# Mixture of experts: weights applied at the eviction, adding gathers, stores on ScalarE's queue, one loop for the rare blocks

## The chip, the cores and the metric

The kernel runs on one core of a Trainium2 chip. The metric is the time of one execution on the device in microseconds (us), the median of three runs. Beside the runs there is one profiled execution, from which all rows below are taken. TensorE (PE in the profile, PEld for its weight loads), VectorE (DVE), ScalarE (ACT), GpSimd (POOL) and SyncE (SP) run their own instruction streams; a small q behind a name (PEq, SPq) is an engine's sequencer, which takes branches and issues transfers.

## The reference, cut to what matters

Two layers of a model with three sequence mixers and a mixture of experts. The mixers and the projections before and after them don't change. The mixture of experts in each layer picks two of 32 experts for each token, runs them, and adds their results with weights; its input is adaptively normalised, and its sum is gated by a row g2 of the stream and added to ALPHA times the row before it goes through a layer norm. Layer 0 has 512 tokens of two streams, layer 1 has 256 of one.

```python
    weights = jax.nn.softmax(top_logit, -1) * group_w
    expert_id = group_idx[:, None] * EXPERTS_PER_GROUP + top_idx.astype(jnp.int32)
    ...
    def run_block(args):
        tok, e = args
        xb = h_pad[tok]
        hid = jax.nn.silu(xb @ w1[e]) * (xb @ w3[e])
        return hid @ w2[e]

    y = lax.map(run_block, (slot_tok.reshape(n_blocks, MOE_BLOCK), block_expert))
    y = y.reshape(cap, d).astype(F32) * slot_w[:, None]
    return jnp.zeros((n_tok + 1, d), F32).at[slot_tok].add(y)[:n_tok].astype(h.dtype)
```

## The kernel before

The tokens' assignments to experts, two for each token, are sorted by expert into slots (1024 in layer 0, 512 in layer 1). `permute` builds one-hot matrices on VectorE and GpSimd and multiplies by them, so that the normalised rows stand in slot order, transposed, in `XS`. `pos` is a slot's number, `posi` the row of the scratch tensor `ysD` in DRAM in which that slot's result lies; `ysD` has NR parts, which the experts take in turn.

An expert works on blocks of RB = 64 slots. `expert_steps` gives the steps of a block: `rows` copies the block's columns of `XS` to `xt`, `up` multiplies them with w1 and w3 (L1616), `gate` is Silu and a product (L1621, L1622), `turn` transposes the result on TensorE (L110, copied by L1628), `down` multiplies with w2 (L1636). `down` then copies the result from PSUM to `yo` on ScalarE (L1638) and stores it to `ysD` by a transfer that GpSimd issues (L1639). `expert_block` is all steps of one block in a row. `e` runs over the experts in a loop that is written out, with the first half of the next expert's `up` moved ahead of `turn` and `down`; expert 0 has code of its own ahead of it.

How many slots an expert has is known only at run time, so the engines load the count (L1653) and branch. Every expert runs one block. `If(cnt > RB)` (L1721) guards a second block written out, and in it `If(cnt > 2 * RB)` (L1724) guards a loop for the rest (L1725). Of the 62 experts behind expert 0 in the two layers, 4 have more than 64 slots here, none more than 128. Behind the If, `reload(e)` issues on SP's queue the loads (L1356) of the weights that go into the buffers which expert e has left free; an expert has six pieces of 1 MB, and some fifteen pieces are held.

Behind the last expert, GpSimd fetches each token's two results by indirect gathers into `yg` (L1738). ScalarE multiplies the first by its weight (L1742), VectorE adds the second times its weight (L1745), GpSimd or VectorE multiplies by the gate row (L1746), VectorE adds ALPHA times the row X (L1747), and `normalise` works on pairs of 128-token blocks (L377 to L384). In layer 0 the next layer's mixers follow: TensorE transposes the rows (L110). The first three loads of their weights are held back by `late`, on ScalarE's queue, until the combination of block 2. In layer 1 the final norm and the store of the output follow.

Of the kernel before, what the change touches and what calls it, by code (L numbers as in the profile page):

```python
# [10 lines left out]
F32 = mybir.dt.float32  # L11
# [70 lines left out]
def backbone(ctx: ExitStack, tc: tile.TileContext, a, out, dbg=None, upto=None):  # L82
# [75 lines left out]
    late = {"n": 0, "ins": None}  # L158
# [253 lines left out]
    for l in range(NLAYER):  # L412
# [5 lines left out]
        late["n"] = 3 if l else 0  # L418
# [1005 lines left out]
        wgt = pe.tile([P, 2, nb], F32, name="wgt")  # L1424
# [28 lines left out]
        for s in streams:  # L1453
# [10 lines left out]
            ls_ = pr.tile([P, CTX], F32, name="ls", tag="o1", bufs=2)  # L1464
# [73 lines left out]
        def permute(q):  # L1538

            on = pr.tile([P, nb, QT], F32R, name="on", tag="on", bufs=2)  # L1540
            for b in range(nb):
                o1 = pr.tile([P, QT], F32, name="o1", tag="o1", bufs=2)
                eng = nc.gpsimd if b % 2 else nc.vector
                eng.tensor_scalar(o1, io, posq[:, 0, b, q:q + 1], None, op0=OP.is_equal)
                nc.vector.scalar_tensor_tensor(on[:, b], io, posq[:, 1, b, q:q + 1], o1, op0=OP.is_equal, op1=OP.add)
            for kp in range(0, KD, 2):
                ps = ps_tile([P, 2, QT], "pj")
                for i in range(2):
                    for b in range(nb):
                        for x in range(2):  # L1550
                            mm(ps[:, i], h2r[(b0 + b) // 2, kp + i][x][:, b % 2], on[:, b], start=(b == 0 and x == 0),
# [6 lines left out]

        for b in blocks:
# [12 lines left out]
        for i in range(2):  # L1572
# [3 lines left out]
            nc.vector.tensor_add(posi[:, i], pos[:, i], rofs)  # L1576

# [10 lines left out]
        nc.vector.tensor_mul(wgt[:, 0], gw, den)  # L1588
        nc.vector.tensor_mul(wgt[:, 1], wgt[:, 0], e2)

        WHY = "a slot is counted once, so start and count stay within the slots"
        def block_tiles(px, tag, n, ny, static=0):

            return {k: px.tile(shp, F32, name=k, tag=tag + k, bufs=ny if k == "yo" else n)
                    for k, shp in (("xt", [P, KD, RB]), ("hd", [P, 256]), ("hh", [P, 2, P]), ("yo", [P, 512]))[static:]}

        def expert_steps(tl, e, off, piece=None):
# [4 lines left out]
            grp = [slice(g * RB, (g + 1) * RB) for g in range(2)]  # L1602
            t = {}

# [14 lines left out]
            def gate():  # L1619
                hd = tl["hd"]  # L1620
# [3 lines left out]
            def turn():  # L1624
                pt = ps_tile([P, 2, P])
                for j in range(2):
                    transpose(pt[:, j], tl["hd"][:, j::2])
                nc.vector.tensor_copy(tl["hh"], pt)  # L1628

            def down():  # L1630
                py = ps_tile([P, 512], "pj")
                for f in range(2):
                    for j in range(2):
                        k = 2 * f + j
                        for g in range(2):
                            mm(py[grp[g]], tl["hh"][:, j, grp[f]], w2(k, g * 512, 512), start=(k == 0), stop=(k == 3),  # L1636
# [144 lines left out]
```

## Time and profile before

| | us |
|---|---|
| runs, median of 3 (lowest to highest) | 2803.15 (2794.74 to 2810.39) |
| profiled execution, time | 2788.21 |
| its span | 2786.6 |
| PE, DVE, ACT, POOL busy | 2209.7, 1158.0, 664.0, 612.6 |
| TensorE's granted clock, mean | 0.905 |

The span is from the first to the last instruction that the profiler saw. Busy time of an engine is the sum over its instructions; two engines' busy times overlap. A row of a timeline gives start, duration, engine, line, operation, output and input, and in brackets the engine's idle time before it with what ended it.

### The profile page before, as it was taken

The numbers are of one execution on the slowest core, as the hardware profiler recorded it, in microseconds if no ns is written. First come the engines' busy times: TensorE is split into PE (matmuls) and PEld (weight loads), VectorE is DVE, ScalarE is ACT, GpSimd is POOL, SyncE is SP. The second block draws the span as 40 slices with busy tenths as digits, with TensorE's granted clock in tenths as the row PEclk, the third lists the DMA queues.
The fourth block names the chain that finished last, engine by engine and source line by source line (L and its number), as shares of the span: only waits on it lengthen the run. The fifth ranks groups of instructions, "written<-read, shape, count | busy, mean of one in ns | idle before, by whom it ended". The sixth has DMA issues, their size and how long they took to land. (4 is left out here: it accounts for less than half of the span.)

```text
span 2786.6 us, 42100 instructions
## 1 busy us (share of the span) xinstructions
PE 2209.7 (79%) x16239; PEld 1551.1 (56%) x16239; DVE 1158.0 (42%) x2451; ACT 664.0 (24%) x1308; POOL 612.6 (22%) x542
## 2 busy tenths in 40 slices
PE   7998988888898887777773899986878687678773
PEld 3666975677685644334331576874777443344331
DVE  4749445876456100000003779467864300000002
ACT  2421345443422100000001342345433100000000
POOL 1242110544333000000002242223554200000001
PEclk9998999999999999899887899998988898898886
DMA  9475451323765488999996258343357769999994
GB/s 316 153 215 171 130 167 42 100 76 103 206 213 197 176 345 318 362 408 408 353 382 219 62 164 262 112 154 87 92 167 241 291 248 381 352 400 408 407 389 157
DMA packets 350438, 657.22 MB, mean 236 GB/s; under 512 B 73462, under 2 KB 253214, under 8 KB 306808
## 3 DMA queue, kind: packets, MB, share of 16 engines
q1 hardware_dynamic: 287890, 599.97, 59.4%
q0 software_dynamic: 38160, 24.63, 2.9%
q10 hardware_dynamic: 24022, 27.84, 2.9%
q8 instruction: 218, 3.57, 0.5%
q14 instruction: 148, 1.21, 0.1%
HBM read 593.09 MB, written 59.02 MB: 234 GB/s over the span
## 5 line engine op out<-in xcount | busy, mean ns | idle before, releaser
L1616 PE MATMUL ps<-we,xt 128*64 128x256 f32 x4224 | 569.6, 423 | 240.5 <-PEq L1721 147.4
L1616 PEld LDWEIGHTS ps<-we,xt 128*64 128x64 f32 x4224 | 339.0, 152 | 458.2 <-issue 329.0
L209 PE MATMUL ps<-hT,whi 128*128 128x512 f32 (+2 forms) x880 | 327.1, 372 | 2.1 <-ACT whi L152 1.9
L154 POOL TENSOR_TENSOR wlo<-raw,whi 128x1024 fp32r<-128x1024 f32 (+1 forms) x84 | 206.2, 2455 | 543.6 <-ACT whi L152 453.2
L211 PE MATMUL ps<-hT,wlo 128*128 128x512 f32 (+2 forms) x880 | 317.2, 360 | 0.3 <-DVE wlo L154 0.3
L210 PE MATMUL ps<-hT,whi 128*128 128x512 f32 (+2 forms) x880 | 317.3, 361 | 0.0
L1639 POOL DMA_DIRECT2D ysD<-yo x69 | 55.6, 806 | 1074.7 <-ACT yo L1638 954.0
L1636 PE MATMUL ps<-we,hh 128*64 128x512 f32 x1104 | 251.9, 597 | 5.2 <-DVE hh L1628 2.6
L152 ACT ACTIVATE whi<-raw 128x1024 fp32r<-128x1024 f32 x174 | 180.1, 1044 | 221.9 <-PE ps L210 158.9
L1638 ACT ACTIVATE yo<-ps 128x512 f32<-128x512 f32 x69 | 41.2, 597 | 798.7 <-PE ps L1636 769.9
L1610 DVE COPY xt<-XS 128x512 f32 x66 | 28.2, 427 | 483.2 <-PE ps L1616 479.0
L1628 DVE COPY hh<-ps 128x256 f32<-128x256 f32 x69 | 29.3, 425 | 409.7 <-PE ps L110 409.7
L209 PEld LDWEIGHTS ps<-hT,whi 128*128 128x128 f32 (+1 forms) x880 | 172.0, 195 | 42.4 <-issue 12.6
L211 PEld LDWEIGHTS ps<-hT,wlo 128*128 128x128 f32 (+1 forms) x880 | 171.4, 195 | 31.4 <-issue 6.9
L210 PEld LDWEIGHTS ps<-hT,whi 128*128 128x128 f32 (+1 forms) x880 | 171.9, 195 | 25.0 <-issue 3.3
L154 DVE TENSOR_TENSOR wlo<-raw,whi 128x1024 fp32r<-128x1024 f32 x90 | 148.1, 1647 | 44.6 <-ACT whi L152 38.8
L1636 PEld LDWEIGHTS ps<-we,hh 128*64 128x64 f32 x1104 | 79.5, 138 | 135.2 <-issue 118.8
L210 PE MATMUL ps<-wlo,hT 128*128 128x256 f32 x384 | 110.1, 287 | 1.5 <-DVE wlo L154 1.5
L209 PE MATMUL ps<-whi,hT 128*128 128x256 f32 x384 | 110.9, 289 | 0.0
L211 PE MATMUL ps<-whi,hT 128*128 128x256 f32 x384 | 109.7, 286 | 0.0
L288 PE MATMUL ps<-wmod,sT 128*32 128x256 f32 x768 | 90.0, 521 | 14.0 <-DMA wmod<-in_w_mod 11.5
L1621 ACT ACTIVATE hd<-ps 128x256 f32<-128x256 f32 x69 | 26.4, 383 | 249.9 <-PE ps L1616 249.9
(423 smaller groups left out, 3718.6 us busy)
## 6 DMA issues: line engine op xcount, KB each, us to landing
we<-in_w SPq DMA_DIRECT2D x338, 1024.0 KB
raw<-in_w_in SPq DMA_DIRECT2D x121, 512.0 KB
wmod<-in_w_mod SPq DMA_DIRECT2D x96, 512.0 KB
we<-in_w SPq DMA_DIRECT2D x92, 512.0 KB
ysD<-yo POOLq DMA_DIRECT2D x69, 256.0 KB, 16.2
ysD<-X SPq DMA_DIRECT2D x17, 512.0 KB
raw<-in_w_out SPq DMA_DIRECT2D x16, 512.0 KB
mgD<-st ACTq DMA_DIRECT2D x24, 256.0 KB
```

The costliest lines, as they stand in the source:

```text
L152: nc.scalar.activation(hr[:, :, off:off + pn], rv, AF.Copy)
L154: eng.tensor_sub(lr[:, :, off:off + pn], rv, hr[:, :, off:off + pn])
L209: mm(ps, st[0](k), mv[0](k), start=(k == 0), stop=False)
L210: mm(ps, st[0](k), mv[1](k), start=False, stop=False)
L211: mm(ps, st[1](k), mv[0](k), start=False, stop=(k == kt - 1))
L288: mm(hold["ps"][32 * j:32 * j + 32, :], sT[:, k, :], cols, start=(k == 0), stop=(k == KD - 1 and v not in mod_d[l]))
L1610: nc.vector.tensor_copy(t["xt"], XS[:, :, ds(off, RB)])
L1616: mm(t["ph"][grp[g], i], t["xt"][:, k], (w1, w3)[i](k, g * 256, 256), start=(k == 0), stop=(k == KD - 1), tile_position=(0, g * RB))
L1628: nc.vector.tensor_copy(tl["hh"], pt)
L1636: mm(py[grp[g]], tl["hh"][:, j, grp[f]], w2(k, g * 512, 512), start=(k == 0), stop=(k == 3), tile_position=(0, g * RB))
L1638: nc.scalar.activation(tl["yo"], py, AF.Copy)
L1639: nc.gpsimd.dma_start(ysD[e % NR, ds(off, RB)].rearrange("s (g c) -> g s c", g=2), tl["yo"])
```

## The change

Four edits, all in the mixture of experts.

1. Each slot's weight is written to a scratch tensor `wsD` in DRAM by indirect transfers of GpSimd, one for each 128 tokens and choice (8 in layer 0, 4 in layer 1), with a zero tail. In layer 0 a slot has two weights, one for each stream, one of them zero. Each block loads its 64 weights twice, to both halves of `wc`, on ScalarE's queue.
2. `down` multiplies by the weight and by the gate row g2 on VectorE where the result leaves PSUM (in layer 0 once for each stream, and adds the two), and the store to `ysD` is issued by ScalarE.
3. The gathers add their rows to X in the transfer itself, first all first choices, then all second ones. ALPHA goes into the rows of the norm that makes X. The combination on ScalarE, VectorE and GpSimd is gone, `late` with it.
4. The second block and the loop behind it become one loop over all blocks beyond the first.

```diff
-            if late["n"]:
-                late["n"] -= 1
-                with tc.issue_after(late["ins"]):
-                    nc.scalar.dma_start(dst, v)
-            else:
-                nc.sync.dma_start(dst, v)
+            nc.sync.dma_start(dst, v)
...
+        wsD = dram.tile([ns + RB, nst], F32, name=f"wsD{l}")
+        g2 = [pe.tile([P, 512], F32, name=f"g2_{s}") for s in streams]
...
+        nc.gpsimd.tensor_scalar(lnrow, lnrow, ALPHA, None, op0=OP.mult)
...
+        nc.scalar.dma_start(wsD[ns:ns + RB], XS[0:RB, 0, ns:ns + nst])
+        for i in range(2):
+            for b in range(nb):
+                nc.gpsimd.indirect_dma_start(out=wsD, out_offset=bass.IndirectOffsetOnAxis(ap=posw[:, i, b:b + 1], axis=0),
+                                             in_=wgt[:, i, b], in_offset=None)
...
+            def weights():
+                for g in range(2):
+                    nc.scalar.dma_start(tl["wc"][grp[g]], wsD[ds(off, RB)])
...
-                nc.scalar.activation(tl["yo"], py, AF.Copy)
-                nc.gpsimd.dma_start(ysD[e % NR, ds(off, RB)].rearrange("s (g c) -> g s c", g=2), tl["yo"])
+                for x in range(nst):
+                    nc.vector.scalar_tensor_tensor(tl["hd" if x else "yo"], py, tl["wc"][:, x:x + 1], g2[x], op0=OP.mult,
+                                                   op1=OP.mult)
+                if nst > 1:
+                    nc.vector.tensor_add(tl["yo"], tl["yo"], tl["hd"])
+                nc.scalar.dma_start(ysD[e % NR, ds(off, RB)].rearrange("s (g c) -> g s c", g=2), tl["yo"])
...
             with tc.If(cnt > RB, label=f"beyond{l}_{e}", preferred_fallthrough_block=True):
-                to = block_tiles(px, *ZO)
-                expert_block(to, e, more(off + RB))
-                with tc.If(cnt > 2 * RB):
-                    with tc.For_i(2 * RB, cnt, RB) as i:
-                        expert_block(to, e, more(off + i))
+                with tc.For_i(RB, cnt, RB) as i:
+                    expert_block(block_tiles(px, *ZO), e, more(off + i))
             reload(e)
...
-            ins = nc.scalar.activation(y0, y0, AF.Copy, scale=wgt[:, 0, b:b + 1])
-            if b == 2:
-                late["ins"] = ins.ins
-            nc.vector.scalar_tensor_tensor(y0, y1, wgt[:, 1, b:b + 1], y0, op0=OP.mult, op1=OP.add)
-            (nc.vector if b == nb - 1 else nc.gpsimd).tensor_mul(y0, y0, g2[(b0 + b) // 2])
-            nc.vector.scalar_tensor_tensor(X[:, b0 + b], X[:, b0 + b], ALPHA, y0, op0=OP.mult, op1=OP.add)
-            if b % 2:
-                normalise([b0 + b - 1, b0 + b])
+        for i in range(2):
+            for b in range(nb):
+                nc.gpsimd.indirect_dma_start(out=X[:, b0 + b], out_offset=None, in_=ysD.rearrange("r s c -> (r s) c"),
+                                             in_offset=bass.IndirectOffsetOnAxis(ap=posi[:, i, b:b + 1], axis=0),
+                                             compute_op=OP.add)
+        for b in range(0, nb, 2):
+            normalise([b0 + b, b0 + b + 1])
```

How the streams stand to each other is seen at three places. The first is GpSimd in the routing stage of layer 0, in the changed kernel, with what each instruction waits for: `on` are the one-hot matrices of `permute`, DMASW0 to DMASW6 are the semaphores of GpSimd's own transfers, in the order of their issue.

```order
L1599 DMA wsD_7579<-wgt,posw 1088x2 [waits DMAHW6_49,DVE_49]
L1599 DMA wsD_7579<-wgt,posw 1088x2 [waits DMASW0_49]
L1542 TENSOR_SCALAR on<-io,posq 128x256 [waits PE_49]
L1599 DMA wsD_7579<-wgt,posw 1088x2 [waits DMASW1_49,DVE_49]
L1542 TENSOR_SCALAR on<-io,posq 128x256 [waits PE_49]
L1599 DMA wsD_7579<-wgt,posw 1088x2 [waits DMASW2_49]
L1599 DMA wsD_7579<-wgt,posw 1088x2 [waits DMASW3_49,DVE_49]
L1599 DMA wsD_7579<-wgt,posw 1088x2 [waits DMASW4_49]
```

These transfers are new. Each waits for the one issued before it, and two one-hot matrices stand between them.

The second is ScalarE at the first block of layer 0, in the changed kernel: L1687 are the branches for expert 0's rare blocks, DMASW7 is the semaphore of the last of those eight transfers.

```order
L1687 COMPARE_AND_BRANCH
L1621 DMA wc<-wsD_7579 64x2 [waits DMAHW5_49,DMASW7_49]
L1621 DMA wc<-wsD_7579 64x2 [waits DMAHW6_49]
L1638 ACT_TABLE_LOAD
L1638 ACTIVATE hd<-ps 128x256 [waits PE_49]
L1661 DMA ysD<-yo 2x64x512 [waits DMAHW7_49,DVE_49]
```

The two loads of weights and their waits now stand ahead of the table load and the Silu; the copy `yo` is gone from this queue and the store has come to it.

The third is the branch behind an expert. First TensorE in the kernel before, from the load of the count to the end of the loop's matmuls:

```order
L1653 TENSOR_LOAD cnt_i
L1721 COMPARE_AND_BRANCH
L1616 MATMUL ps<-we,xt 64x256 x32
L110 MATMUL ps<-cst,hd 128x128 x2
L1636 MATMUL ps<-we,hh 64x512 x8
L1724 COMPARE_AND_BRANCH
L1725 COMPARE_AND_BRANCH
L1725 UNCONDITIONAL_BRANCH x2
L1777 BRANCH_PREFETCH_HINT
L1616 MATMUL ps<-we,xt 64x256 x32
L110 MATMUL ps<-cst,hd 128x128 x2
L1636 MATMUL ps<-we,hh 64x512 x8
```

And in the changed kernel:

```order
L1676 TENSOR_LOAD cnt_i
L1746 COMPARE_AND_BRANCH
L1747 COMPARE_AND_BRANCH
L1747 UNCONDITIONAL_BRANCH x2
L1790 BRANCH_PREFETCH_HINT
L1634 MATMUL ps<-we,xt 64x256 x32
L110 MATMUL ps<-cst,hd 128x128 x2
L1653 MATMUL ps<-we,hd 64x512 x8
L1747 REGISTER_ALU
L1747 COMPARE_AND_BRANCH
L1747 UNCONDITIONAL_BRANCH
L1746 UNCONDITIONAL_BRANCH
```

One copy of a block is gone from between the branch and its target, and the second block of an expert is now reached through the entry of a loop. On SP the same entry of the loop, in the changed kernel, reads as follows; the second row lists all queues' semaphores (DMASW of GpSimd's, DMAHW of SP's and ScalarE's) and those of the engines:

```order
L1746 COMPARE_AND_BRANCH
L1747 COMPARE_AND_BRANCH
L1747 UNCONDITIONAL_BRANCH [waits DMAHW2_49,DMAHW3_49,DMAHW4_49]
L1747 UNCONDITIONAL_BRANCH [waits DMASW4_49,DMASW3_49,DMASW5_49,DMASW2_49,DMASW6_49,DMASW1_49,DMASW7_49,DMASW0_49,DMAHW0_49,SP_sequencer_49,DMAHW1_49,DVE_sequencer_49,DMAHW2_49,PE_sequencer_49,DMAHW3_49,Activation_sequencer_49,DMAHW4_49
L1790 BRANCH_PREFETCH_HINT
L1747 REGISTER_ALU
L1747 COMPARE_AND_BRANCH
```

A loop of this form stood in the kernel before too (L1725), behind two branches; it is not entered there with these counts, and it is now entered four times.

## Rows read from the trace of the kernel before

**Rows 1.** Table of stretches: us, busy PE PEld DVE ACT POOL, PEclk, DMA share, GB/s
```profile
900.00:940.00 40.00, 36.35 (x281) 25.84 (x281) 7.12 (x15) 5.43 (x9) 5.38 (x8) 1.00 0.50 190
1060.00:1180.00 120.00, 87.05 (x557) 45.20 (x556) 8.82 (x21) 6.86 (x14) 5.59 (x7) 0.87 0.95 370
1180.00:1305.00 125.00, 95.57 (x646) 50.65 (x648) 9.25 (x22) 7.46 (x15) 6.37 (x8) 0.92 1.02 407
1305.00:1435.00 130.00, 93.95 (x586) 48.74 (x584) 8.82 (x21) 6.86 (x14) 5.58 (x7) 0.83 0.93 366
2330.00:2475.00 145.00, 105.99 (x684) 55.56 (x682) 9.67 (x23) 8.44 (x17) 7.17 (x9) 0.87 0.93 365
```

**Rows 2.** The line of the branch: durations in ns, then who waited
```profile
L1721 PEldq COMPARE_BRANCH  x62: 70/3387/7289, 966.8 to 2738.4; - x62
...
  PE ps L1616: 159.0, 38
```

**Rows 3.** Timeline of TensorE, layer 0, behind a long branch
```profile
1348.67 3.68 PE L1616 MATMUL ps<-we,xt 128*64 128x256 f32 x16 [5.25 <-PEq L1721]
```

**Rows 4.** Timeline of the fronts of both layers
```profile
891.53 0.15 DVE L1589 TENSOR_TENSOR wgt<-wgt,e 128x4 f32<-128x4 f32 x1
...
907.04 0.38 ACT L1621 ACTIVATE hd<-ps 128x256 f32<-128x256 f32 x1 [9.54 <-PE ps L1616]
...
2188.47 2.37 DVE L1589 TENSOR_TENSOR wgt<-wgt,e 128x2 f32<-128x2 f32 x1
...
2203.45 0.38 ACT L1621 ACTIVATE hd<-ps 128x256 f32<-128x256 f32 x1 [9.48 <-PE ps L1616]
```

**Rows 5.** The line of the gathers, us from issue to landing
```profile
DMA to landing us min/median/max: 4.3/5.7/6.5
```

**Rows 6.** Timeline, start of layer 1's mixers
```profile
1531.77 0.43 SPq L124 DMA_DIRECT2D db<-in_gdn_dt_bias  x1
...
1534.03 1.28 ACT L551 ACT_TABLE_LOAD   x1 [9.08 <-DMA db<-in_gdn_dt_bias]
```

**Rows 7.** Timeline of TensorE around three blocks beyond 64 slots
```profile
998.76 7.13 PE L1616 MATMUL ps<-we,xt 128*64 128x256 f32 x64 [1.64 <-DVE xt L1610]
...
1044.03 7.13 PE L1616 MATMUL ps<-we,xt 128*64 128x256 f32 x64 [1.97 <-DVE xt L1610]
...
1057.72 1.95 PE L1616 MATMUL ps<-we,xt 128*64 128x256 f32 x16 [0.96 <-ACTq L1724]
...
2275.90 7.13 PE L1616 MATMUL ps<-we,xt 128*64 128x256 f32 x64 [1.63 <-DVE xt L1610]
```

**Rows 8.** Table of stretches around those blocks
```profile
1000.00:1010.00 10.00, 8.55 (x68) 5.42 (x66) 0.85 (x2) 0.38 (x1) 0.00 (x0) 1.00 0.42 161
...
1040.00:1050.00 10.00, 8.03 (x76) 5.92 (x74) 1.26 (x3) 0.38 (x1) 0.40 (x1) 1.00 0.65 258
...
2280.00:2290.00 10.00, 7.89 (x55) 4.04 (x51) 0.85 (x2) 0.98 (x2) 0.38 (x1) 1.00 0.54 204
```

**Rows 9.** The line of the stores, us from issue to landing
```profile
DMA to landing us min/median/max: 8.6/16.2/21.2
```

**Rows 10.** Timeline of the end of layer 0
```profile
1490.22 0.80 POOL L1639 DMA_DIRECT2D ysD<-yo  x1 [9.38 <-ACTq L1721]
1500.40 1.07 POOL L1738 DMA_INDIRECT yg<-ysD,posi  x1 [9.38 <-issue]
...
1538.07 3.93 PE L110 MATMUL ps<-cst,X 128*128 128x128 f32 x16 [48.83 <-DVE X L384]
```

**Rows 11.** Timeline of the end of layer 1
```profile
2743.85 0.80 POOL L1639 DMA_DIRECT2D ysD<-yo  x1 [10.70 <-ACTq L1721]
...
2755.74 1.05 POOL L1738 DMA_INDIRECT yg<-ysD,posi  x1 [11.10 <-DMA ysD<-yo]
...
2768.57 0.69 DVE L377 BATCH_NORM_STATS2 bst<-X 128x6 f32<-128x512 f32 x1
...
2776.27 1.53 DVE L384 TENSOR_SCALAR X<-X,bve,bnm 128x1024 f32<-128x1024 f32 x2
```

More of the change, by code (lines that the diff above doesn't have):

```diff
@@ L1538, in permute @@
         def permute(q):
-            on = pr.tile([P, nb, QT], F32R, name="on", tag="on", bufs=2)
+            on = [pr.tile([P, QT], F32R, name="on", tag="on", bufs=nb + 2) for _ in range(nb)]
             for b in range(nb):
-                o1 = pr.tile([P, QT], F32, name="o1", tag="o1", bufs=2)
                 eng = nc.gpsimd if b % 2 else nc.vector
-                eng.tensor_scalar(o1, io, posq[:, 0, b, q:q + 1], None, op0=OP.is_equal)
-                nc.vector.scalar_tensor_tensor(on[:, b], io, posq[:, 1, b, q:q + 1], o1, op0=OP.is_equal, op1=OP.add)
+                eng.tensor_scalar(on[b], io, posq[:, 0, b, q:q + 1], None, op0=OP.is_equal)
+                nc.vector.scalar_tensor_tensor(on[b], io, posq[:, 1, b, q:q + 1], on[b], op0=OP.is_equal, op1=OP.add)
             for kp in range(0, KD, 2):
@@ L1550, in permute @@
                         for x in range(2):
-                            mm(ps[:, i], h2r[(b0 + b) // 2, kp + i][x][:, b % 2], on[:, b], start=(b == 0 and x == 0),
+                            mm(ps[:, i], h2r[(b0 + b) // 2, kp + i][x][:, b % 2], on[b], start=(b == 0 and x == 0),
                                stop=(b == nb - 1 and x == 1))
@@ L1576, in backbone @@
             nc.vector.tensor_add(posi[:, i], pos[:, i], rofs)
+        posw = pr.tile([P, 2, nb], I32, name="posw")
+        nc.vector.tensor_copy(posw, pos)
+        wgt = pr.tile([P, 2, nb, nst], F32, name="wgt")
+        nc.gpsimd.memset(wgt, 0.0)
+        own = [wgt[:, i, 2 * x:2 * x + 2, x] for i in range(2) for x in range(nst)]
         eg = pr.tile([P, nb, NG], F32, name="eg")
@@ L1602, in expert_steps @@
             grp = [slice(g * RB, (g + 1) * RB) for g in range(2)]
+            hd, hh = tl["hd"][:, :256], tl["hd"][:, 256:].rearrange("p (j s) -> p j s", j=2)
             t = {}
+            def weights():
+                for g in range(2):
+                    nc.scalar.dma_start(tl["wc"][grp[g]], wsD[ds(off, RB)])
             def rows():
@@ L1626, in turn @@
                 for j in range(2):
[L1627 to L1628 removed]
+                    transpose(pt[:, j], hd[:, j::2])
+                nc.vector.tensor_copy(hh, pt)
             def down():
@@ L1635, in down @@
                         for g in range(2):
-                            mm(py[grp[g]], tl["hh"][:, j, grp[f]], w2(k, g * 512, 512), start=(k == 0), stop=(k == 3),
+                            mm(py[grp[g]], hh[:, j, grp[f]], w2(k, g * 512, 512), start=(k == 0), stop=(k == 3),
                                tile_position=(0, g * RB))
-                nc.scalar.activation(tl["yo"], py, AF.Copy)
-                nc.gpsimd.dma_start(ysD[e % NR, ds(off, RB)].rearrange("s (g c) -> g s c", g=2), tl["yo"])
-            return rows, up, gate, turn, down
+                for x in range(nst):
+                    nc.vector.scalar_tensor_tensor(tl["hd" if x else "yo"], py, tl["wc"][:, x:x + 1], g2[x], op0=OP.mult,
[3 more added lines that the diff above has]
+                nc.scalar.dma_start(ysD[e % NR, ds(off, RB)].rearrange("s (g c) -> g s c", g=2), tl["yo"])
+            return rows, up, gate, turn, down, weights
         def expert_block(*args):
-            rows, up, gate, turn, down = expert_steps(*args)
+            rows, up, gate, turn, down, weights = expert_steps(*args)
+            weights()
             rows()
@@ L1705, in backbone @@
         for e in range(1, NE):
-            rows, up, gate, turn, down = steps.pop(e)
+            rows, up, gate, turn, down, _ = steps.pop(e)
             tc.mark_branch_hint_location(f"beyond{l}_{e}", "LikelyTaken")
```

30 lines of the change are left out of this document (12 added, 18 removed).

## The prediction

> **What bounds the kernel now.** The expert stage runs from about 900 to 1490 us in layer 0 and from 2190 to 2745 us in layer 1, so it is two fifths of the time, and all of the change lies in it and at its two ends. I read the table of stretches first [rows 1]. In 1180 to 1305 the DMA share is 1.02 at 407 GB/s: that is the ceiling, and the experts' weights set the pace there. In 1060 to 1180 the share is 0.95, in 1305 to 1435 0.93, in 2330 to 2475 0.93, so there something else holds the loads up for a part of the time. What it is, the line of the branch tells [rows 2]: TensorE's branch behind each expert took 0.07 us at best, 3.4 in the median and 7.3 at worst, on the same test each time, and the next expert's matmuls waited 159 us for it. In the long case TensorE sits idle 5.25 us and its next 16 matmuls take 3.68 us [rows 3], against 1.95 for 16 such matmuls in a run that is not interrupted [rows 7]: it comes back slower, and the granted clock of the stretch is 0.83 against 0.92 where the loads set the pace [rows 1]. The branch is taken over code that is not run, and what is jumped over is the block beyond 64 and the loop behind it, two copies of a block. That one and the same test takes so differently long says that the code at the target is sometimes at hand and sometimes has to be brought.
>
> The two ends are chains of waits: last result, store, gathers, combination, normalisation, and TensorE idle over all of it, 48.83 us behind layer 0 [rows 10] and to the end of the program behind layer 1 [rows 11]. The front is a chain too: routing, weights, first block [rows 4].
>
> **The change part by part.** The profiled execution took 2788.2 us, the median of the runs is 2803.15, 0.5% above. I add up differences on the profile and put them on the median.
>
> *Weights by slot (front of each layer).* After the weights are known (VectorE, 891.7 us [rows 4]), GpSimd writes them to DRAM with 8 indirect transfers in layer 0 and 4 in layer 1. Each waits for the one before it to land, as the order shows, since all write one tensor. ScalarE's load of the first block's weights waits for the last of them, and behind that load on ScalarE's queue stand the table load and the first Silu, for which all of TensorE waits. No row has such a transfer. From below a small transfer of the hardware queue, 1531.77 to 1534.03, 2.3 us [rows 6]; from above the indirect gathers, 4.3 to 6.5 us [rows 5]. It moves 8 bytes a row where the gather moves 4 KB, so I take 3.8, just under the shortest gather. Layer 0: 891.7 + 8 x 3.8 = 922.1, two loads issued at about 0.4 each [rows 6] and a table load of about 1.3 behind it: Silu at 924 in place of 907.04, **+17** (2.3 us each: +5; 5.7 each: +32). Layer 1: 2190.8 + 4 x 3.8 = 2206 + 2 = 2208 against 2203.45 [rows 4]: **+4.5** (0 to +12). It is not made up later: the DMA share in 900 to 940 is 0.50 [rows 1], that is, the weights prefetched are in their buffers and nothing can be loaded until an expert is done.
>
> *The multiplication where the results leave PSUM.* One copy on ScalarE becomes three operations on VectorE in layer 0, one in layer 1. At 0.69 us for 128x512 [rows 11] that is 2.1 us. VectorE is busy 9 of 120 us [rows 1], and the next matmuls into that bank come an expert later: nothing, but for the last block, where it adds 1.5 us ahead of the store (counted below). The scaling of the norm's row by GpSimd and the earlier loads of the gate's rows lie in the routing stage, in which GpSimd waits; nothing. The first loads of layer 1 on SP's queue: nothing, since SP has issued all experts by then.
>
> *The loop for slots beyond 64.* It is run 4 times here: twice in layer 0 (from 998.76 and 1044.03), twice in layer 1 (one at 2275.90) [rows 7]. Now such a block is straight code; after one of them TensorE stood idle 0.96 us [rows 7]. In the changed kernel it is the body of a loop, and the order shows at its entry and its exit a wait of SP for the semaphores of all DMA queues and all engines, and a release of all engines together. At the entry SP waits until the weights under way have landed. They kept the DMA engines busy 4.2 us from 1000, 6.5 us from 1040 and 5.4 us from 2280 [rows 8], which is up to 5.4, 2.5 and 9.5 us after the blocks' starts; for the fourth I count none: 17 in all. At the exit the block's store has to land (2.3 to 8.6 us [rows 6, 9]; 3), after the multiplications (2), and entry and exit are each a meeting of five engines with a branch; a branch costs from 0.07 to 7.3 [rows 2], I take 1.5 for each meeting. That is 8 each, 32 in all. While this lasts no weights are issued, since SP stands in the same loop. **+49**; between 4 each with nothing under way, +16, and 15 each, +77.
>
> *The branch.* What is jumped over is halved: the order shows one block copy less between the branch and its target. I take it that the target is then nearly always at hand. What that is worth is not the branch's time but the time that the DMA engines lose by it, against 1.02: 0.07 x 120 + 0.09 x 130 + 0.09 x 145 = 33 us [rows 1]. I take **-28**, since the other engines' entry into an expert keeps some of it; between 0 and -33.
>
> *Stores on ScalarE's queue.* On GpSimd's queue a store landed after 8.6 to 21.2 us, 16.2 in the median [rows 9]. Within the stage nobody waits for it. At the ends the first gather does: 1490.22 to 1500.40 and 2743.85 to 2755.74 [rows 10, 11]. On the other queue I take 3 us, near the small transfer's 2.3 [rows 6], plus 1 us issue. Gain 10.2 - 4 - 1.5 = 4.7 and 11.9 - 4 - 0.1 = 7.8, which are part of the two ends' sums below. [...]
>
> *Gathers that add.* ScalarE's, VectorE's and GpSimd's combination falls away; normalisation stays. Normalisation is some 9 us for a pair (2768.57 to 2777.8 with three other operations between [rows 11]). Layer 0: gathers from 1495.8; the first four take 1.1 to 1.3 us each to issue, the second four may follow at once, since the first has landed by then (5.7 us [rows 5]); the sixth is issued at 1503, lands at 1509, and the first pair is normalised at 1517 to 1518 against TensorE's restart at 1538.07 [rows 10]: with the store **-20**. Layer 1: gathers from 2748, the second two wait for the first two: 2754 to 2756.5, landed at 2762, normalised at 2769 to 2771 against 2777.8: **-9** with the store. No row shows a gather that adds. It has one operand more to bring, so from above twice as long: -10 and -3; from below as a plain gather with a quicker normalisation: -25 and -13.
>
> Sum: 17 + 4.5 + 49 - 28 - 20 - 9 = **+13.5**: 2802 for the profiled execution, **2816** on the median.
>
> **The rivals.** *The loop is cheap* (the one on the other side). The weights under way are all landed at the entry, and meetings cost little: 4 us an event. Then 21.5 + 16 - 33 - 34 = -30: 2773. It is decided at 8 us an event, over four events: under that the kernel is faster if the ends gain what a plain gather gives. For it: the shares in front of two of the events are low [rows 8]. Against it: the store inside the loop must land before anyone goes on, and that has a floor of 2.3 us [rows 6] before any meeting.
> *The branch stays long or the adding gathers are slow.* If bringing code is set by the jump as such, the 28 don't come; if adding doubles the gathers, the ends give 13 rather than 29. Both: 21.5 + 49 - 13 = +58: 2861; one of them, 2832 to 2844. For it: adding is not in any row.
> *The stores are hidden or no quicker on the other queue*: the ends give 12 less, 2828. [...]
> *SP is held up by shared semaphores.* Loads of weights, two loads of slot weights and one store per expert now share the 8 semaphores of the hardware queues; a load may wait for a store to land. At 1.5 us for each of 58 experts: +87, 2900. [...]
>
> **How the numbers follow.** What a measurement of this kernel can tell from no change is about 0.5%, 14 us: 2789 to 2817. The forecast, drains and front outweighing branch and ends by a little, 2795 to 2840 (with the stores' rival in it): 0.43. The cheap loop, 2765 to 2790: 0.28. Slow gathers, long branches or drains of 15 us, 2840 to 2870: 0.20. SP held up, above that: 0.09. Range 2762 to 2870. Faster by over 0.5%: the cheap loop and little else, 0.29; within: half of the forecast and the cheap loop's upper edge, 0.27; slower: 0.44.
>
> **What would show it.** In the changed profile: branch rows of TensorE under 0.5 us nearly throughout, and the DMA share at 1.02 between the events; a gap of some 20 us of TensorE ahead of the first Silu of layer 0, with eight indirect writes in it one behind the other; around the four events 8 to 20 us in which neither TensorE nor the DMA engines work, with SP waiting for weights; TensorE's restart about 28 us after layer 0's last block. I am wrong if the loop's events cost under 4 or over 20 us each, if the scatters go out without waiting, if adding gathers take over 10 us to land, or if the share of DMA stays under 1 between events.

## The result: slower by 15%, and the profile after

The changed kernel takes 3230.25 us (3225.52 to 3242.24), the kernel before 2798.94 with the runs made beside it; the ratio is 1.154, 95% interval 1.151 to 1.158. That is 431 us, where 13.5 were forecast and 2870 was the upper end of the range. The profiled execution has a span of 3223.7 us. Medians are of the runs at the usual granted clock; one run of the control with two tensors on GpSimd's queue, 3601 us at a clock of 0.57, is left out.

The table of stretches of the changed kernel, with the columns of [rows 1]:

```profile
1180.00:1305.00 125.00, 80.64 (x446) 38.78 (x444) 18.92 (x33) 1.92 (x5) 0.00 (x0) 0.75 0.74 282
1305.00:1435.00 130.00, 78.87 (x460) 39.18 (x458) 18.07 (x33) 2.31 (x6) 0.00 (x0) 0.82 0.72 273
2700.00:2900.00 200.00, 124.80 (x690) 64.79 (x692) 17.43 (x35) 3.46 (x9) 0.00 (x0) 0.77 0.73 279
```

The share of the DMA engines is not 1.02 and not 0.93 but 0.72 to 0.74, in steady stretches of both layers. TensorE is busy less, so it isn't TensorE that the weights wait for. The branch is not the reason either; its line, and who waits on SP (the second fence: engine and line, whom it waited for, us in all, times, longest):

```profile
L1746 PEldq COMPARE_BRANCH  x62: 70/330/586, 987.2 to 3176.7; - x62
```

```profile
SPq L1348 <- DMA ysD<-yo: 516.9, 54, 14.0
...
SPq L1348 <- DMA we<-in_w: 420.8, 85, 8.6
```

The branch is short throughout (0.07 to 0.59 us against 3.4 in the median before [rows 2]), as forecast. But SP, which issues the weights' loads, has waited 517 us for the stores to land, a wait that the kernel before doesn't have. One expert, in the timelines of the engines (L1653 is `down`):

```profile
1317.61 3.82 PE L1653 MATMUL ps<-we,hd 128*64 128x512 f32 x16
1321.32 1.95 PE L1634 MATMUL ps<-we,xt 128*64 128x256 f32 x16
1323.64 1.09 ACTq L1661 DMA_DIRECT2D ysD<-yo  x1
...
1333.00 3.68 PE L1634 MATMUL ps<-we,xt 128*64 128x256 f32 x16 [7.16 <-DMA we<-in_w]
...
1339.63 3.60 PE L1653 MATMUL ps<-we,hd 128*64 128x512 f32 x16
```

From one `down` to the next it is 22.0 us, and TensorE stands 7.16 us before weights. At the two ends, which answer to [rows 10, 11], first layer 0, then layer 1:

```profile
1714.83 1.08 ACTq L1661 DMA_DIRECT2D ysD<-yo  x1
...
1725.80 1.64 POOL L1758 DMA_INDIRECT X<-ysD,posi  x1 [763.89 <-DMA raw<-in_w_in]
...
1757.57 4.18 PE L110 MATMUL ps<-cst,X 128*128 128x128 f32 x16 [44.96 <-DVE X L377]
...
3180.46 1.07 ACTq L1661 DMA_DIRECT2D ysD<-yo  x1
...
3192.22 1.64 POOL L1758 DMA_INDIRECT X<-ysD,posi  x1 [751.65 <-DMA ysD<-yo]
...
3212.45 1.53 DVE L377 TENSOR_SCALAR X<-X,bve,bnm 128x1024 f32<-128x1024 f32 x2
```

The first gather comes 11.0 and 11.8 us after the issue of the last store. On GpSimd's queue it was 10.2 and 11.9 [rows 10, 11]: with the store written as it was, ScalarE's queue is no quicker. (In layer 0 the row names a load of w_in as what ended the wait.) The landing row of the line of the gathers, which now add, then that of the indirect writes of the slot weights, then the front of layer 0 in the timeline:

```profile
DMA to landing us min/median/max: 6.3/9.2/11.1
```

```profile
DMA to landing us min/median/max: 2.1/2.5/6.4
```

```profile
891.41 1.21 POOL L1599 DMA_INDIRECT wsD<-wgt,posw  x1 [1.56 <-DVE wgt L1595]
...
917.45 1.19 ACTq L1621 DMA_DIRECT2D wc<-wsD  x2
918.67 1.28 ACT L1638 ACT_TABLE_LOAD   x1 [22.55 <-issue]
919.97 0.38 ACT L1638 ACTIVATE hd<-ps 128x256 f32<-128x256 f32 x1
```

The chain of eight writes holds up the first Silu as forecast: 919.97 against 907.04 [rows 4]. In layer 1 not only the Silu stands behind the load of the slot weights, but TensorE's `up` ahead of it too:

```profile
2409.48 0.15 DVE L1595 TENSOR_TENSOR wgt<-wgt,e 128x2 f32<-128x2 f32 x1
...
2431.51 8.43 PE L1634 MATMUL ps<-we,XS 128*64 128x256 f32 x64 [16.81 <-DMA wc<-wsD]
2439.99 0.38 ACT L1638 ACTIVATE hd<-ps 128x256 f32<-128x256 f32 x1 [7.19 <-PE ps L1634]
```

The Silu comes 30.4 us after the weights are known, against 12.6 [rows 4].

### The profile page after: what moved, and what is told of

It is laid out like the page before. It is cut to its first block, busy times and chain, and to the rows that moved or that the text cites. A ratio compares the mean times of both kernels' runs of the same rounds, so it can differ in the third digit from the quotient of the medians.

```text
span 3223.7 us, 42855 instructions
## 1 busy us (share of the span) xinstructions
PE 2337.4 (73%) x16239; PEld 1595.2 (49%) x16239; DVE 1238.9 (38%) x2580; ACT 615.9 (19%) x1233; POOL 572.5 (18%) x485
## 5 line engine op out<-in xcount | busy, mean ns | idle before, releaser
L1634 PE MATMUL ps<-we,xt 128*64 128x256 f32 x4224 | 665.0, 464 | 513.3 <-DMA we<-in_w 369.6
L1634 PEld LDWEIGHTS ps<-we,xt 128*64 128x64 f32 x4224 | 372.8, 165 | 785.3 <-issue 501.3
L1758 POOL DMA_INDIRECT X<-ysD,posi x12 | 19.7, 1644 | 1525.0 <-DMA raw<-in_w_in 763.9
L1653 PE MATMUL ps<-we,hd 128*64 128x512 f32 x1104 | 278.6, 644 | 6.0 <-DVE hd L1645 5.2
L1657 DVE SCALAR_TENSOR_TENSOR yo<-ps,wc,g 128x512 f32<-128x512 f32 x69 | 51.8, 751 | 559.7 <-PE ps L1653 503.7
L1645 DVE COPY hd<-ps 128x256 f32<-128x256 f32 x69 | 29.3, 425 | 478.9 <-PE ps L110 460.6
L202 PEld LDWEIGHTS ps<-hT,whi 128*128 128x128 f32 (+1 forms) x880 | 172.3, 196 | 42.6 <-issue 13.5
L1653 PEld LDWEIGHTS ps<-we,hd 128*64 128x64 f32 x1104 | 89.3, 155 | 161.9 <-issue 146.3
```

The source lines that it names most:

```text
L202: mm(ps, st[0](k), mv[0](k), start=(k == 0), stop=False)
L1634: mm(t["ph"][grp[g], i], t["xt"][:, k], (w1, w3)[i](k, g * 256, 256), start=(k == 0), stop=(k == KD - 1), tile_position=(0, g * RB))
L1645: nc.vector.tensor_copy(hh, pt)
L1653: mm(py[grp[g]], hh[:, j, grp[f]], w2(k, g * 512, 512), start=(k == 0), stop=(k == 3), tile_position=(0, g * RB))
L1657: nc.vector.scalar_tensor_tensor(tl["hd" if x else "yo"], py, tl["wc"][:, x:x + 1], g2[x], op0=OP.mult, op1=OP.mult)
```

## The theories

Two things can make the weights late. Both follow from the store's move to ScalarE's queue.

Theory A, two engines. The store is written as `ysD[...].rearrange("s (g c) -> g s c", g=2)`: the slowest dimension of its pattern in DRAM is 2. The theory is my inference from this pattern and the rows: the store is on two of the 16 DMA engines, and from ScalarE's queue on the same two each time. An expert's weights are 6.29 MB, a sixteenth is 0.393; the store's 0.262 MB put 0.131 on each of the two, 0.524 together, 1.33 times as much. The whole 6.55 MB at the 407 GB/s of [rows 1] are 16.1 us; 0.524 MB at a sixteenth of 407 GB/s are 20.6, beside 22.0 in the rows above. Two engines full and fourteen at three quarters are a share of 0.78, beside 0.72 to 0.74. On GpSimd's queue the same store stands beside a share of 1.02 [rows 1], so there it can't be on the same two each time.

No view of the profile shows the engines one by one, but the share of a short stretch tells how many of them work. After the store that ScalarE issues at 1305.03, these are a stretch of the changed kernel, what moved in it on ScalarE's queue (q10: packets, MB, share) and on SP's (q1), and SP's wait, which ends at 1316.33:

```profile
1312.00:1316.00 4.00, 1.83 (x12) 1.01 (x12) 0.42 (x1) 0.00 (x0) 0.00 (x0) 0.83 0.13 51
...
q10 hardware_dynamic: 85, 0.12, 8.1%
q1 hardware_dynamic: 13, 0.08, 4.9%
...
SPq L1348 <- DMA ysD<-yo: 9.0, 1, 9.0
```

A share of 0.13 is two engines of sixteen. They finish the store and a rest of the weights at 51 GB/s, while fourteen are idle and SP stands before its next load. So the low mean isn't level: it is made of stretches at the ceiling and of such ones. Of the 260 us from 1180 to 1440, taken one by one, 47 have a share between 0.05 and 0.2 in the changed kernel and none in the kernel before. The trace shows the two engines; what they cost, and whether the pattern or the queue is to blame, takes experiments.

Theory B, shared semaphores. In the orders of the streams SP's and ScalarE's transfers share the semaphores DMAHW0 to DMAHW7, and in the fence above SP stands 9.0 us before a load of weights until the store has landed. In all that is 517 us in 54 waits, the longest 14.0, against none in the kernel before. The load issued at 1316.33 has the same semaphore as the store of 1305.03. So a load whose semaphore a store used last would wait for that store, the longer the later it lands. This was the last rival of the prediction.

## The experiments

All times are medians; ratios are to the kernel before, run on the same chip.

### Store as two halves on ScalarE's queue, store on GpSimd's queue, and the same moves in the kernel before

In the changed kernel the two halves:

```diff
-                nc.scalar.dma_start(ysD[e % NR, ds(off, RB)].rearrange("s (g c) -> g s c", g=2), tl["yo"])
+                for g in range(2):
+                    nc.scalar.dma_start(ysD[e % NR, ds(off, RB), g * 512:(g + 1) * 512], tl["yo"][grp[g]])
```

> The changed kernel, with the store of a block's result issued by ScalarE as two transfers of 64 partitions in place of one of 128 (same bytes, same queue, one more transfer on the shared semaphores). Theory A (two engines): the one store is written with a leading dimension of 2 on the DRAM side and is carried by two of the 16 DMA engines, the same two each time; for each expert these two move 131 KB beside their sixteenth of 6.29 MB, 0.524 MB instead of 0.393, and the weights, which need all 16, come at 4/3 of 16 us. Split by 64 partitions the store spreads, and the time falls to 2770 to 2840. Theory B (shared semaphores): SP's loads wait because a store holds a semaphore of the hardware queues until it lands; with one more transfer in the round the time stays at 3200 or above.

Measured: 2919.0, ratio 1.042 (1.039 to 1.045). The same bytes on the same queue, with one more transfer on the semaphores, and 311 of the 431 us are gone. The pattern is the larger part, but theory A alone is too little: its range ended at 2840.

> The changed kernel with the store put back on GpSimd's queue as it was. Both theories: the store no longer loads the same two engines and no longer takes a semaphore of the hardware queues, so the loss goes: 2780 to 2850, the other edits by my sum (front +17, loop +49, branch -28, ends -16 without a quicker store) at about 2820. If neither theory is right (the slot weights' loads or the eviction on VectorE hold the stage up) it stays above 3000.

The edit is `nc.scalar` to `nc.gpsimd` in that one line. Measured: 2884.9, ratio 1.028 (1.025 to 1.032), 35 above the range.

> The kernel before with nothing changed but the store's engine: ScalarE instead of GpSimd. Theory A: 62 experts times up to 5.3 us, less what the long branches hide: 3030 to 3150. Theory B: with no slot weights on the hardware queues seven transfers an expert share eight semaphores, so a load waits for a store more rarely: 2850 to 2950.

The edit is `nc.gpsimd` to `nc.scalar` in L1639. Measured: 3063.2, ratio 1.094 (1.089 to 1.099). The move of one line costs the kernel before 261 us, within theory A's range; SP's wait for stores, of which theory B speaks, is there too. The stretch of 1180 to 1440 in this kernel (52 of its 260 us have a share between 0.05 and 0.2), and then SP's wait:

```profile
1180.00:1440.00 260.00, 162.71 (x984) 82.37 (x984) 15.14 (x36) 11.78 (x24) 0.00 (x0) 0.79 0.74 292
```

```profile
SPq L1356 <- DMA ysD<-yo: 705.2, 57, 17.6
```

> The kernel before with the store on ScalarE's queue as two transfers of 64 partitions. Theory A: no loss, and the two ends gain if a spread store lands in 3 us instead of 10: 2770 to 2805. Theory B: as with the one store or above, 2850 to 3000.

Measured: 2907.7, ratio 1.038 (1.034 to 1.041): 105 us are left with a spread store, which theory B would have. But ScalarE's timeline shows something that neither theory spoke of:

```profile
2593.89 0.60 ACT L1638 ACTIVATE yo<-ps 128x512 f32<-128x512 f32 x1 [9.74 <-PE ps L1636]
2594.52 7.71 ACTq L1640 DMA_DIRECT2D ysD<-yo  x2
2602.68 0.38 ACT L1621 ACTIVATE hd<-ps 128x256 f32<-128x256 f32 x1 [8.19 <-DMA we<-in_w]
```

The two halves take 7.71 us to issue, where one takes 0.48: the second waits for the first to land. Both write the same tensor, at an offset that is known only at run time; that this keeps them in order is a guess. The next expert's Silu stands behind them and can't start before 2602.23, though its row names the weights. What the Silu waited for stores in all (us, times), here and in the run with two tensors that follows below:

```profile
ACT hd L1621: 84.4, 12
...
ACT hd L1622: 20.0, 7
```

So this run and the first have a cost of their own, theory C.

### Stores and slot weights on GpSimd's queue, and the straight block

> The kernel before with its store on GpSimd's queue, as two transfers of 64 partitions instead of one of 128. Theory A (the one store runs on two DMA engines, on GpSimd's queue on a different two each time): a spread store lands earlier, so the first gather at both ends starts some 5 us sooner: 2780 to 2800 against 2802. If the landing is set by the queue (software against hardware) and not by the number of engines: 2800 to 2810.

Measured: 2769.1, ratio 0.988 (0.983 to 0.993), 11 below theory A's range. The line of the stores, now of one half each, has this to set against [rows 9]; the second row is from the run below with two tensors on this queue:

```profile
DMA to landing us min/median/max: 2.2/6.1/7.8
...
DMA to landing us min/median/max: 2.2/6.9/8.2
```

A half lands in 6 to 7 us. Here the second half is issued only when the first has landed (GpSimd waited 393.7 us for that, 66 times), so the whole store takes some 12 us; with two tensors, at 0.52 us for an issue, the whole 256 KB take some 7.5 by estimate, instead of 16.2 on the same queue. What set its landing was its pattern, not the queue. At the two ends the first gather comes only 2.1 and 2.6 us sooner after the last store than in [rows 10, 11], not 5; most of the 31 us lies within the stage.

> The changed kernel with the store on GpSimd's queue as two transfers of 64 partitions; the slot weights' loads stay on ScalarE's queue. Against the kernel with one store on GpSimd's queue (2885) this shows the spread alone, against the run with everything on GpSimd's queue the two small loads' share of the semaphores. Theory A: 5 us earlier at both ends and less uneven load: 2860 to 2880. Theory B': 20 to 40 above the run with everything on GpSimd's queue.

Measured: 2795.7, ratio 0.999 (0.997 to 1.002), 64 below theory A's range. Written as one transfer on the same queue the store had cost 89 us more in this kernel (2884.9), where it was 31 in the kernel before; so the pattern costs something on GpSimd's queue too, though in 1180 to 1440 of the kernel before no microsecond has a share between 0.05 and 0.2. Why it is more here is not shown. In 1180 to 1440 the DMA share is back at the ceiling:

```profile
1180.00:1440.00 260.00, 201.84 (x1348) 106.37 (x1346) 54.22 (x97) 6.13 (x16) 16.68 (x32) 0.90 1.02 414
```

> The changed kernel with the two loads of slot weights of each block and the store (as two transfers of 64 partitions) on GpSimd's queue, so that in the expert stage only the weights' loads use the semaphores of the hardware queues. Theory B' (what is left of the loss once the store is spread comes from the shared semaphores): the DMA share of the steady stretches returns from 0.93 to 0.99 to 1.02 and the time to 2820 to 2850, that is, my sum for the other edits. If the semaphores have no part in it: as with the store alone on GpSimd's queue, 2870 to 2890.

Measured: 2799.0, ratio 0.999 (0.997 to 1.001), below both ranges. With or without the slot weights on the hardware queues it is the same: two small loads an expert on shared semaphores cost nothing that can be told. The 20 to 40 that theory B' expected are not there.

> The changed kernel with slot weights and spread store on GpSimd's queue, and the second block of an expert written out again with the loop behind a second test, as before the change. By my prediction's terms (loop +49, shorter branch -28) it is 21 us faster than the same kernel with the one loop, and TensorE's branch shows 3 to 7 us again in half of the experts. By the rival of the cheap loop (4 us an event) it is 15 to 30 us slower.

The edit puts the lines of the diff's loop back as they were. Measured: 2817.5, ratio 1.006 (1.004 to 1.009), 18 us slower than with the one loop, and the branch is long again:

```profile
L1747 PEldq COMPARE_BRANCH  x62: 70/3388/7440, 980.4 to 2759.6; - x62
```

So the one loop gains, as the rival of the cheap loop had it, where my terms for it and the branch made +21 together.

### What is left on ScalarE's queue when halves don't wait

Two tensors, one for each half of the columns, take away the wait of the second half; the gathers fetch halves.

```diff
-    ysD = dram.tile([NR, YROWS, D], F32, name="ysD")
+    ysH = [dram.tile([NR, YROWS, 512], F32, name=f"ysD{g}") for g in range(2)]
...
+                for g in range(2):
+                    nc.scalar.dma_start(ysH[g][e % NR, ds(off, RB)], tl["yo"][grp[g]])
```

> The kernel before with its results in two tensors in DRAM, one for each half of the columns, so that the two half stores (64 partitions each) don't wait for one another, issued by ScalarE; the gathers fetch halves, twice as many. Compared with the same kernel with the stores on GpSimd's queue. Theory B (shared semaphores): SP's loads wait for the stores: 2850 to 2910. Theory C (what was left of the loss with two halves on ScalarE's queue came from ScalarE standing before its second store until the first had landed, ahead of the next Silu): 2770 to 2800.

> The control for the run with two tensors and stores on ScalarE's queue: the same, stores on GpSimd's queue. Against one tensor with two halves on GpSimd's queue (2769): the second half no longer waits for the first at the ends (4 us each), but 8 and 4 more gathers are issued at about 1.2 us: 2765 to 2785.

> The kernel with two tensors, its main blocks' stores on SP's queue, issued behind the reloads of the expert's weights, when the result has long been copied; the rare blocks' stores on GpSimd's queue. Same hardware queues and semaphores as with ScalarE, but in one order, so that no load waits for a store that isn't issued yet. Theory B: the loss goes, 2765 to 2800. If stores on a hardware queue cost as such (the transfers themselves, not the waits for them): as with ScalarE.

Measured: 2819.5 on ScalarE's queue (ratio 1.005, 1.003 to 1.008), 2768.7 on GpSimd's (0.987, 0.983 to 0.990), 2767.8 on SP's behind the reloads (0.986, 0.983 to 0.989). On ScalarE's queue it falls between theory C's range and B's, below the 2850 that B gave. The hardware queue as such costs nothing here (SP against GpSimd, 0.9 us apart). ScalarE against GpSimd is 51 us, and SP's rows have a wait that the run on GpSimd's queue lacks: with ScalarE

```profile
SPq L1357 <- DMA ysD<-yo: 227.5, 41, 26.6
```

SP has waited 228 us for stores; in the run with late stores on SP's own queue no weights' load has such a row. That is theory B, at up to 51 us with a spread store; ScalarE's own time for two issues an expert, about 0.5 us each, is in it too and was not taken apart. From two halves in one tensor (2908) to two tensors (2820), 88 us go: theory C.

> The changed kernel with its results in two tensors, stored by ScalarE as two transfers of 64 partitions each, which don't wait for one another; adding gathers of halves, twice as many. Only the spread over the DMA engines differs from the change in the steady stage. Theory A for the larger part: 2840 to 2870, that is 360 to 390 of the 431 us are the two engines' and the rest is SP's wait for stores (47 in the kernel before) and the slower gathers. If the shared semaphores are the larger part in this kernel, with two more small loads in the round: 2900 to 3100.

Measured: 2856.6, ratio 1.022 (1.016 to 1.028). In the changed kernel itself the spread gives back 374 of 431 us, without a change of queue or of semaphores' number in its favour. (The 47 that the expectation takes from the kernel before is 51 by the medians above.) The share in 1180 to 1440, where 1 of the 260 us now has a share between 0.05 and 0.2, and SP's wait:

```profile
1180.00:1440.00 260.00, 185.40 (x1244) 98.18 (x1246) 50.59 (x90) 5.75 (x15) 0.00 (x0) 0.89 0.99 388
```

```profile
SPq L1349 <- DMA ysD<-yo: 272.2, 90, 8.0
```

So the pattern on ScalarE's queue is the cause. How it acts the runs don't take apart: the weights' own bytes wait on the two engines, and SP waits for a store that lands late because of them (517 us before the spread, 272 with it). The stretch at 1312 above shows both at once. A store on two engines that SP issues behind its own loads would tell them apart; no run has it.

### The loop alone, and the front and the ends

> The kernel before with the store on GpSimd's queue as two transfers of 64 partitions, and the second block and the loop behind it as one loop; nothing else of the change. The straight form cost 18 us more than the loop in the changed kernel; if that is the loop's whole worth, this kernel takes 2745 to 2760, and TensorE's branches stay under 1 us. By my prediction's terms (loop +49, branch -28) it would be 2780 to 2795.

Measured: 2759.0, ratio 0.982 (0.979 to 0.986), the best of all runs: the kernel before with two edits, and faster than either kernel. Against the same kernel with the straight block (2769.1) it is 10 us faster in the medians, though the two intervals overlap a little. TensorE's timelines split it into its parts; `down` of the first block of layer 1, of the expert behind the last block beyond 64 and of the last expert, first with the straight block, then with the loop:

```profile
2201.63 3.65 PE L1636 MATMUL ps<-we,hh 128*64 128x512 f32 x16 [0.56 <-issue]
...
2288.78 3.60 PE L1636 MATMUL ps<-we,hh 128*64 128x512 f32 x16
...
2723.25 5.35 PE L1636 MATMUL ps<-we,hh 128*64 128x512 f32 x16 [0.52 <-DVE hh L1628]
```

```profile
2196.87 3.65 PE L1636 MATMUL ps<-we,hh 128*64 128x512 f32 x16 [0.56 <-issue]
...
2301.34 3.60 PE L1636 MATMUL ps<-we,hh 128*64 128x512 f32 x16
...
2719.14 3.65 PE L1636 MATMUL ps<-we,hh 128*64 128x512 f32 x16 [0.56 <-issue]
```

To the second row it is 87.2 us straight and 104.5 with the loop: the two loops cost 17.3, some 9 each, less what the short branches between them gave. From there to the end it is 434.5 and 417.8: the short branches give 16.7 back in this layer.

> The changed kernel with the store on GpSimd's queue as two halves (2796), and in expert_block the load of the slot weights behind the gate, so that ScalarE does the first block's Silu before it waits for the last indirect write. Theory: the 13 us by which the first Silu of layer 0 came late, and some 4 in layer 1, go, since nothing else waits for the slot weights before the eviction: 2776 to 2788. If the eviction itself then waits for them as long: 2790 to 2800.

Measured: 2796.8, ratio 0.999 (0.997 to 1.001), no change. The edit didn't reach the engine's stream: in ScalarE's timeline the load of the slot weights still stands ahead of the table load and the Silu. So this run says nothing of the front. The run with everything on GpSimd's queue says something: there the first Silu comes at 911.19, against 921.86 with the slot weights on ScalarE's queue, but the time is no shorter (2799.0 against 2795.7), and VectorE waits for the slot weights in the Silu's stead:

```profile
922.24 0.75 DVE L1657 SCALAR_TENSOR_TENSOR yo<-ps,wc,g 128x512 f32<-128x512 f32 x1 [9.19 <-DMA wc<-wsD]
```

> The kernel of the run before with plain gathers into tiles of their own and two additions on VectorE for each 128 tokens in place of gathers that add. Theory (a gather that adds is issued in 1.5 us and lands after 9, a plain one 0.94 and 5.7, and the second to one row has to wait for the first): 10 to 20 us faster, 2760 to 2775. If the additions on VectorE take as long as the slower gathers: within 5 us of the run before.

Measured: 2790.4, ratio 0.996 (0.994 to 0.999), 6 us below the run before it, with intervals that touch: a gain at the edge of what can be told, and smaller than expected. By the profiles TensorE's wait at the end of layer 0 is 37.95 us, against 42.89 in the run before it.

## Why the prediction was wrong

**The step that failed** is the store's move. I wrote "Within the stage nobody waits for it" and took 12.5 us as its gain, in the two ends' sums. In the changed kernel SP, which issues the weights' loads, waited 517 us for it, and its bytes shared two of the sixteen engines with those loads, by the share of 0.13 at 1312. It cost nearly all of the 431: the spread of the store in the changed kernel gives back 374 (3230 to 2857), and from there to two halves on GpSimd's queue (2796) it is 61, the stores on shared semaphores together with twice as many gathers. In the kernel before, the move of a spread store to ScalarE's queue measured 51. I looked at how long the store takes and who waits for its data, and not at how its bytes are laid on the engines, and what else these engines carry.

**Where it could be read.** [Rows 9] show 256 KB that take 8.6 us at best, and when the stage is over it is still 10 to 12 to the first gather [rows 10, 11]; at the ceiling of [rows 1] all engines together move that in 0.64. A transfer that takes 13 times its share of the bandwidth may run on few engines. I took all of it for the queue's price and hoped for 3 us.

**Queue and pattern.** The 4 us that I took for the store on the other queue, 3 and 1 for the issue, no run shows: from the last store to the first gather it is 11.0 and 11.8 us on ScalarE's queue, against 10.2 and 11.9 on GpSimd's [rows 10, 11]. My rows could not tell the queue from the pattern. The runs do: two halves give 311 us back on ScalarE's queue, 374 where the halves don't wait.

**The rivals.** SP held up by shared semaphores was on the list, at 87 us and a chance of 0.09. Its mechanism is real: up to 51 us in the kernel before with a spread store, and with the store on two engines a part of the 374 that is not split off. I named a store's landing there as what a load may wait for, but put it at 1.5 us for each expert, with the landing of a store that only its own bytes delay; in the rows above one such wait is 9.0 us. Its low chance counted on loads under way to keep the engines busy behind a late issue, which no row shows. At 1312 they didn't: only the rests on the two engines were under way, at a share of 0.13. (The rival of the cheap loop took -34 for the ends, where the terms above it give -29, and -38 at best.)

**Front, loop, branch, ends.**
- Front: +17 forecast for layer 0, 12.9 in the rows; eight writes took 26 us from the first's issue to the load behind them, 3.3 each, where I took 3.8. In layer 1 +4.5 was forecast, 12 at most, and it is 17.8 in the rows (30.4 against 12.6): I had only the table load and the Silu behind the load, and `up` stood behind it too.
- The loop: +49 forecast, 17.3 for the two loops of layer 1, so about 35 for four if layer 0's cost as much (in the kernel before, with the spread store). The mechanism (SP waits for all landings, engines meet) was right, with 94.7 us of SP's waits for stores and 19.6 for weights at L1747 of the changed kernel, and each event was taken too dear.
- The branch: TensorE's rows came out as said, -28 forecast, -16.7 in layer 1 alone. The share of the DMA engines between events went to 1.01 in the run with the loop alone.
- Together: -10 and -18 in two pairs of runs, where I had +21. The sign of that sum was wrong.
- Ends: TensorE restarts 45 us after its last matmul of layer 0, against 48.83 [rows 10]. I forecast about 28. Layer 0's end gained 3.9 us where I had 20, layer 1's 0.4 where I had 9 (2743.85 to 2776.27 [rows 11], 3180.46 to 3212.45 now). Of that 4.7 and 7.8 were to come from the store's queue, which gave nothing. A gather that adds is issued in 1.54 to 2.57 us and lands after 9.2, against 1.07 [rows 10] and 5.7 [rows 5], and the one to the same row waits for it. That is on the way to my upper bound, twice as long, and I had taken the time of a plain one.

With the same store, two halves on GpSimd's queue, the changed kernel is 27 us above the kernel before (2795.7 against 2769.1), and my sum without the store's term was +26. That is luck. Loop and branch came out 31 to 39 us below my terms. The rest, fronts and ends, came out as much above: with the same store and the same loop it is 37 us (2795.7 against 2759.0), where I had +5.

The profiles of these last two runs are 27.6 us apart, and they say where it lies; the first Silu of each layer, first in the kernel before with spread store and loop, then in the changed one with spread store:

```profile
912.90 0.38 ACT L1621 ACTIVATE hd<-ps 128x256 f32<-128x256 f32 x1 [9.53 <-PE ps L1616]
...
2194.91 0.38 ACT L1621 ACTIVATE hd<-ps 128x256 f32<-128x256 f32 x1 [8.61 <-PE ps L1616]
```

```profile
921.86 0.38 ACT L1638 ACTIVATE hd<-ps 128x256 f32<-128x256 f32 x1
...
2220.64 0.38 ACT L1638 ACTIVATE hd<-ps 128x256 f32<-128x256 f32 x1 [8.34 <-PE ps L1634]
```

The first Silu of layer 0 comes 9.0 us later, and from the known weights to the first Silu of layer 1 it is 16.6 more: the two fronts are 25.6 of it. The two ends are 4.1 and 3.2 shorter, so the adding gathers don't make the loss. From the first Silu to the last `down` the two layers take 8.1 and 5.1 longer, where the prediction had nothing for the multiplications, and the mixers 3.8 less.

What stays open: what these 13 us within the expert stages are. The change also builds the one-hot matrices of `permute` block by block and puts `hh` into the tile of `hd`, and no run takes that apart. Nor is it shown what the late front is worth by itself: with the first Silu of layer 0 on time the run was no faster.

## What to carry to other kernels

When a transfer moves from one queue to another, ask first whether its bytes sit on few DMA engines, and on the same ones each time; here a store of 4% of the bytes, on two of sixteen engines by the share of 0.13, held up the loads that otherwise keep all sixteen busy (1.02 [rows 1]). A transfer that lands much later than its bytes need is the sign to look for (8.6 us at best [rows 9], where 0.64 would do at the ceiling), and writing it so that its slowest dimension is the 64 rows is the first thing to try: as two halves it gained on either queue here (374 us on ScalarE's, 89 and 31 on GpSimd's). And where the share of the DMA engines is well under 1 while everyone waits for loads, look at it microsecond by microsecond: the steps at 0.13 here are the work of two engines alone. Then see what the issuing engine waits for, since it can be the very transfer on these two.

## What the runs showed of the hardware that was not expected

- The same 256 KB store on the same software queue lands in 16.2 us in the median as one transfer with a slowest dimension of 2. As two transfers of 64 partitions each half lands in 6.1, or in 6.9 where the halves don't wait for one another.
- Some 7 us after such a store on ScalarE's queue the share of the DMA engines falls to 0.13, two of sixteen, at 51 GB/s, for about 4 us, until the store has landed.
- A plain store that is moved from GpSimd's to ScalarE's queue, with nothing else changed, made this kernel 9.4% slower; in two tensors, spread over the engines and issued by SP behind its own loads, it made it 1.4% faster.
- A gather that adds to its target takes 9.2 us to land where a plain one takes 5.7, and 1.54 us or more to issue instead of 0.94.
